# An encoder's FFN: the first two hidden units of each layer are computed like the others, their token differences are formed while the output projection ends, and the last rows' inputs are fetched earlier

## The chip, the cores and the metric

The kernel runs on 1 core of a Trainium2 chip. The time is that of the device in microseconds (us), from three runs; lower is better. The core's engines are TensorE (PE in the profile, with its weight loads as PEld), VectorE (DVE), ScalarE (ACT), GpSimd (POOL) and SyncE (SP). DMAs are issued from SP's, POOL's and, for a few, ACT's queue.

## What is computed

Two layers on 1024 tokens of width 1024, in float32. Each layer has a token mixer (layer 0: window attention; layer 1: a bidirectional gated linear recurrence; both with four cross-attention heads), an output projection, and an FFN, every part with a norm before and after it. The change lies in the FFN and in the end of the output projection.

```python
def conv_ffn(v, w_in, conv_w, conv_b, w_out):
    gate, up = jnp.split(v @ w_in, 2, axis=-1)
    hid = jax.nn.gelu(dwconv_centred(gate, conv_w, conv_b)) * up
    return hid @ w_out
```

w_in is 1024 x 5632 and w_out 2816 x 1024. The convolution runs over tokens, width 3.

## The kernel before

A float32 product is made of three matmuls: each operand is split in a high part (uh, wh; a cast on ACT) and a low part (ul, wl; a subtraction on DVE), and high x high, high x low and low x high are summed in PSUM.

**The FFN's first projection** runs over 22 units f of 128 hidden channels (gate and up together). For 20 of them (f from 2) a Strassen scheme cuts tokens, model width and gate/up in halves each: 7 products instead of 8, each 4 blocks of 128 x 3 matmuls of 128x512, into PSUM tiles X, Y and V (line 541, in mmk). The tokens' halves are i and j. The products' token operands are B[1], B[2], B[3] and B[5] to B[7] with B[4]: B1 to B3 are slices of uh and ul; B5 replaces the slice of the j half, lower four blocks, by a difference to the i half, and B4, B6 and B7 (u4, u6, u7, high and low each) are sums of the others, formed by operands() on DVE. The weights' operands are a raw slice (st), sx and sy (sums of slices, accumulated by DMAs on POOL's queue, lines 636 to 638, from loads on SP's queue, lines 633 and 634) and a second raw slice (a22). sx and sy have two buffers each, so units overlap in pairs.

Units 0 and 1 of each layer are computed by plain(): four PSUM tiles of 8 blocks x 3 matmuls. While PE works on them, operands() runs.

**In front of it** WOut.finish goes over eight row tiles of 128 tokens: the output projection into pb (lines 84 to 86), a norm, the residual (x, line 516), its store to h1d (line 517), and norm_T (line 115 makes nu, line 119 transposes it into pt; the split gives uh and ul). Small norm steps go over POOL (prs and nrs, line 96). PE works through its list in order; SP's, POOL's and ACT's DMAs are issued in the order of each queue, and an issue that waits holds up what is behind it.

**The FFN's second projection** runs seven products in the order 1, 6, 7, 4, 2, 5, 3 over 11 pairs of units, with loads st<-hid and st<-w2s on SP's queue. tail() ends a row tile: it reads the residual x back from h1d (line 800), norms, adds and stores; the first four row tiles during product 5, the last four behind product 3.

What stands in which order on each engine is decided by a scheduler that lists the instructions by their dependencies and priorities; its clock is a model.

Of the kernel before, what the change touches and what calls it, by code (L numbers as in the profile page):

```python
# [6 lines left out]
F32 = mybir.dt.float32  # L7
# [37 lines left out]
PLAIN = 2  # L45

# [3 lines left out]
def build(tc, A, out):  # L50
# [37 lines left out]
    def split(h, l, src):  # L88
        act.copy(h, src)  # L89
        dve.tensor_tensor(l, src, h.bitcast(F32), op=ALU.subtract)  # L90
# [19 lines left out]
    def norm_T(pl, pst, src, g, dh, dl, t, tag="n"):  # L110
        ss = pl.tile([P, 1], F32, tag=tag + "ss", name=tag + "ss")
        u = pl.tile([P, D], F32, tag=tag + "u", name=tag + "u")
        sumsq(pl, src, ss, u)
        rs = rstd_of(pl, ss, 1, D, tag)
        dve.scalar_tensor_tensor(u, src, rs[:, 0:1], g, op0=ALU.mult, op1=ALU.mult)
        for b in range(2):
            ps = pst.tile([P, 4, P], F32, tag="pt", name="pt")
            for k in range(4):
                pe.transpose(ps[:, k, :], u[:, (4 * b + k) * P:(4 * b + k + 1) * P], ident)
            split(dh[:, 4 * b:4 * b + 4, t * P:(t + 1) * P],  # L120
                  dl[:, 4 * b:4 * b + 4, t * P:(t + 1) * P], ps)
# [252 lines left out]
    class WOut:  # L374
# [96 lines left out]
        def finish(self):  # L471
            l = self.l
            self.wf = tc.alloc_tile_pool(name=f"wf{l}", bufs=1, side="right", reuse_waits="tile") if l == 0 else None
# [26 lines left out]
            self.first = wunit(A["ffw1"][l, 0, :, :1024], pl=self.wf) if l == 0 else None  # L500
            for t in self.order:
                pool.tensor_tensor(y0[:, t, :], y0[:, t, :], g1[:, :512], op=ALU.mult)
            for t in self.order:
# [8 lines left out]
                dve.tensor_tensor(y1, ps, g1[:, 512:], op=ALU.mult)  # L512
# [31 lines left out]
    def ffn(l, wo, dst, gnext, halves_, out_halves):  # L544
        u2p = tc.alloc_tile_pool(name=f"u2{l}", bufs=1, reuse_waits="tile")
# [6 lines left out]
        ncw = fp.tile([P, NF, 3], F32, name="ncw")  # L552
        dve.tensor_scalar_mul(ncw, cw, -1.0)
# [23 lines left out]
        def gtile():  # L577
            return fp.tile([P, T], F32, tag="g", bufs=1, name="g")

        def plain(f):  # L580

            wg = wo.first if f == 0 and wo.first else wunit(A["ffw1"][l, f, :, :1024])
            wu = wunit(A["ffw1"][l, f, :, 1024:])
            bank = lambda t: psx.tile([P, 512], F32, tag=t, name=t)
            gi, ui, gj, uj = bank("X"), bank("Y"), bank("V"), bank("Y")
            for (wh, wl), ps, m in ((wg, gi, ti), (wu, ui, ti), (wg, gj, tj), (wu, uj, tj)):
                mmk(ps, KT, lambda k: (wh[:, k * P:(k + 1) * P], wl[:, k * P:(k + 1) * P]),
                    lambda k: (uh[:, k, m], ul[:, k, m]), True)
            g = gtile()
            u = fp.tile([P, T], F32, tag="u", bufs=1, name="u")  # L590
            for gp, up_, m in ((gi, ui, ti), (gj, uj, tj)):
                act.activation(g[:, m], gp, AF.Copy, scale=-1.0)
                act.copy(u[:, m], up_)
            return conv(f, g, u)

        def operands():

            b12 = (uh[:, :4, tj], ul[:, :4, tj])
            late = []
            for kk in range(2):  # L600
                ks = slice(2 * kk, 2 * kk + 2)
                f32 = lambda x: x[:, ks].bitcast(F32)
                def tmp(t, b=1):
                    return fp.tile([P, 2, 512], F32, tag=t, bufs=b, name=t)
                def both(o, x, y, sub):
                    q = tmp("tt", 2)
                    dve.tensor_tensor(o, f32(x[0]), f32(y[0]), op=ALU.subtract)
                    dve.tensor_tensor(q, f32(x[1]), f32(y[1]), op=ALU.subtract)
                    dve.tensor_tensor(o, o, q, op=ALU.add)
                def more(o, a_, x, op):  # L610
                    dve.tensor_tensor(o, a_, f32(x[0]), op=op)
                    dve.tensor_tensor(o, o, f32(x[1]), op=op)
                x = tmp("c", 3)
                both(x, B[3], b12, True)
                split(B[7][0][:, ks], B[7][1][:, ks], x)
                more(x, x, B[1], ALU.add)
                nsplit(B[6][0][:, ks], B[6][1][:, ks], x)
                more(x, x, B[2], ALU.subtract)
                split(B[4][0][:, ks], B[4][1][:, ks], x)
                e1 = tmp("u") if kk else tmp("g")  # L620
                both(e1, B[1], b12, True)
                late.append((ks, e1))
            return late

        def load(f):

            w = A["ffw1"][l, f]
            a1 = stg.tile([P, 1024], F32, tag="st", name="st")
            a22 = stg.tile([P, 1024], F32, tag="st", name="st")[:, :512]
            sx, sy = [fp.tile([P, 1024], F32, tag=t, bufs=2, name=t) for t in ("sx", "sy")]  # L630
            nc.sync.dma_start(a1, w[:, 1024:])
            for c in range(2):
                nc.sync.dma_start(sx[:, c * 512:(c + 1) * 512], w[:, :512])
            nc.sync.dma_start(sy, w[:, 1024:])
            nc.sync.dma_start(a22, w[:, 512:1024])
            pool.dma_start(sx, w[:, 512:1536], accum_op=ALU.add, max_dma_last_dim=8192)
            pool.dma_start(sy[:, :512], sx[:, :512], accum_op=ALU.add, max_dma_last_dim=8192)
            pool.dma_start(sy[:, 512:], sy[:, :512], accum_op=ALU.add, max_dma_last_dim=8192)
            return a1, sx, sy, a22

        def weights(raw):

            for src in raw:
                n = src.shape[-1]
                h, l_ = [ring.tile([P, 1024], F32R, tag=t, name=t)[:, :n] for t in ("wh", "wl")]
                split(h, l_, src)
                yield h, l_
# [36 lines left out]
        def first_units():  # L684
            for f in range(PLAIN):
                c = plain(f)
                if f == 0:
                    late = operands()
                hidden(f, c)
                if f == PLAIN - 1:  # L690
                    for ks, e1 in late:
                        split(B[5][0][:, ks], B[5][1][:, ks], e1)
            raws = {f: load(f) for f in (PLAIN, PLAIN + 1)}
            gen = weights(raws.pop(PLAIN))
            ops = list(gen)
            X = [psx.tile([P, 512], F32, tag="X", name="X")]
            s = {}
# [7 lines left out]
            start(ops)  # L705
            yield
            for f in range(PLAIN, NF):
# [10 lines left out]
                v, y = (psx.tile([P, 512], F32, tag=t, name=t) for t in "VY")  # L718
                w = lambda k: operand(ops, k)
                prod(2, w(2), y, True)  # L720
# [17 lines left out]
                if f + 1 < NF:  # L738
                    X.append(psx.tile([P, 512], F32, tag="X", name="X"))
                    start(nxt)  # L740
# [5 lines left out]
                yield  # L746

# [27 lines left out]
        psx.release()  # L775
        fp.release()
        u2p.release()
        if wo.wf:
            wo.wf.release()
# [10 lines left out]
        y = {q: yp.tile([P, 4, 512], F32, name=q) for q in ("c11", "c21", "c12", "c22")}  # L790
# [37 lines left out]
        for k in SECOND:  # L828
# [4 lines left out]
            for p in range(NP2):  # L833
# [472 lines left out]
```

## Time and profile before

| | us |
|---|---|
| median of three runs | 2729.53 |
| lowest, highest | 2729.33, 2731.97 |
| profiled execution's span | 2732.3 |
| first projection's start, layer 0 | 593.4 to about 640 |
| first projection's start, layer 1 | about 2079 to 2125 |
| second projection's last product, layer 0 | from 1207.3 |
| second projection's last product, layer 1 | from 2690.9 to 2723.1 |

No time of the profiled execution apart from its span is given. Times in rows are microseconds from the start of the span, in groups the mean of one instruction is in ns. A row's bracket gives the idle time of its engine before it and what ended that. PE's records overlap, as matmuls are pipelined; the distance between starts is what one costs.

### The profile page before, as it was taken

How to read it: one execution, taken by the hardware profiler on the slowest of the kernel's cores; microseconds unless marked ns; L12 is line 12 of the kernel's file. 1: busy time of each engine (PE TensorE's matmuls, PEld its weight loads, DVE VectorE, ACT ScalarE, POOL GpSimd, SP SyncE). 2: the span in 40 equal slices, each digit the busy share in tenths (PEclk: the TensorE clock that was granted, in tenths of full speed). 3: DMA queues.
4: the chain of work that ended last, by engine and by line, in shares of the span. 5: the costliest groups of instructions: out<-in, count | busy, mean ns of one | idle time of the engine just before them, and what ended most of it. 6: DMA issues, size and time to landing. Idle time of an engine off the chain costs nothing.

```text
span 2732.3 us, 37483 instructions
## 1 busy us (share of the span) xinstructions
PE 2661.3 (97%) x13496; PEld 2231.1 (82%) x13496; DVE 1824.4 (67%) x3031; ACT 1391.2 (51%) x2550; POOL 468.6 (17%) x517
## 2 busy tenths in 40 slices
PE   8999999999999999999999999999899999999998
PEld 7888887788888888877888888888788788888886
DVE  6588777678556565488686767868566856556456
ACT  6367667544444445455444545545454544444453
POOL 1231120211111100032222231312121111110012
PEclk9999999999999999999999999999999999999999
DMA  8683213656777856673235531111466677775656
GB/s 282 207 186 75 66 49 97 204 183 154 199 205 187 206 155 232 204 249 124 86 124 127 117 78 55 55 47 34 133 219 170 165 202 204 197 206 159 222 192 219
DMA packets 213579, 428.45 MB, mean 157 GB/s; under 512 B 20368, under 2 KB 77072, under 8 KB 207760
## 3 DMA queue, kind: packets, MB, share of 16 engines
q1 hardware_dynamic: 187264, 333.50, 37.8%
q0 software_dynamic: 23680, 88.09, 15.6%
q10 hardware_dynamic: 2448, 4.46, 0.4%
q8 instruction: 106, 1.74, 0.3%
q14 instruction: 81, 0.66, 0.1%
HBM read 333.17 MB, written 117.96 MB: 165 GB/s over the span
## 4 chain that ended last, share of the span: by engine, by line
PE 84%; DVE 8%; DMA 3%; ACT 2%; issue 2%; POOL 1%; SPq 0%; DVEq 0%; POOLq 0%; ACTq 0%
PE X L541 25%; PE V L541 11%; PE pj L84 7%; PE pj L85 7%; PE pj L86 7%; PE Y L541 5%; PE pb L84 4%; PE pb L85 4%; PE pb L86 3%; PE po L1122 1%; PE pt L341 1%; PE pa L1074 1%; PE pa L1054 1%; DVE wl L80 1%; DVE wl L90 1%
## 5 line engine op out<-in xcount | busy, mean ns | idle before, releaser
L90 DVE TENSOR_TENSOR wl<-st,wh 128x1024 fp32r<-128x1024 f32 (+1 forms) x234 | 258.6, 1110 | 338.3 <-ACT wh L89 331.1
L89 ACT CAST wh<-st 128x1024 fp32r<-128x1024 f32 (+1 forms) x234 | 219.1, 938 | 291.4 <-PE X L541 180.4
L84 PE MATMUL pj<-uh,wh 128*128 128x512 f32 x512 | 206.6, 404 | 6.4 <-DVE xl L90 4.6
L541 PE MATMUL X<-wl,wh 128*128 128x512 f32 x528 | 205.6, 391 | 0.6 <-DVE wl L90 0.6
L541 PE MATMUL X<-wh,wl 128*128 128x512 f32 x528 | 205.7, 391 | 0.0
L541 PE MATMUL X<-wh 128*128 128x512 f32 x528 | 201.0, 391 | 4.0 <-DVE c L850 3.8
L86 PE MATMUL pj<-uh,wl 128*128 128x512 f32 x512 | 203.4, 398 | 0.0
L85 PE MATMUL pj<-ul,wh 128*128 128x512 f32 x512 | 202.7, 396 | 0.1
L84 PE MATMUL pj<-wh,uh 128*128 128x384 f32 (+1 forms) x512 | 190.2, 372 | 0.4 <-DVE v L283 0.4
L85 PE MATMUL pj<-wl,uh 128*128 128x384 f32 (+1 forms) x512 | 186.3, 364 | 0.0
L86 PE MATMUL pj<-wh,ul 128*128 128x384 f32 (+1 forms) x512 | 186.1, 364 | 0.0
L80 DVE TENSOR_TENSOR wl<-st,wh 128x1024 fp32r<-128x1024 f32 (+1 forms) x93 | 115.9, 1252 | 28.0 <-ACT wh L79 27.1
L541 PE MATMUL V<-uh,wh 128*128 128x512 f32 x344 | 133.9, 389 | 0.3 <-ACT uh L89 0.3
L541 PE MATMUL V<-ul,wh 128*128 128x512 f32 x344 | 134.0, 389 | 0.0
L541 PE MATMUL V<-uh,wl 128*128 128x512 f32 x344 | 133.9, 389 | 0.0
L79 ACT CAST wh<-st 128x1024 fp32r<-128x1024 f32 (+1 forms) x103 | 104.0, 1016 | 49.0 <-PE pj L85 27.2
L541 PEld LDWEIGHTS X<-wh 128*128 128x128 f32 x528 | 99.5, 189 | 25.9 <-issue 4.6
L84 PEld LDWEIGHTS pj<-uh,wh 128*128 128x128 f32 x512 | 97.3, 190 | 26.6 <-DVE xl L90 5.5
L1068 POOL TENSOR_TENSOR E<-EP,q 128x256 f32<-128x256 f32 x64 | 54.4, 851 | 372.0 <-DVE EP L1061 286.7
L541 PEld LDWEIGHTS X<-wl,wh 128*128 128x128 f32 x528 | 99.5, 189 | 21.9 <-DVE wl L90 1.0
L541 PEld LDWEIGHTS X<-wh,wl 128*128 128x128 f32 x528 | 99.4, 188 | 20.9
L86 PEld LDWEIGHTS pj<-uh,wl 128*128 128x128 f32 x512 | 97.0, 190 | 19.6
(337 smaller groups left out, 7328.7 us busy)
## 6 DMA issues: line engine op xcount, KB each, us to landing
st<-hid SPq DMA_DIRECT2D x154, 256.0 KB, 3.4
st<-in_ffw_dram SPq DMA_DIRECT2D x106, 256.0 KB, 3.5
w2s<-in_ffw_dram POOLq DMA_DIRECT2D x24, 1024.0 KB, 8.0
st<-in_ffw_dram SPq DMA_DIRECT2D x48, 512.0 KB, 3.7
hid<-tt SPq DMA_DIRECT2D x88, 256.0 KB, 4.6
st<-w2s SPq DMA_DIRECT2D x88, 256.0 KB, 3.2
sx<-in_ffw_dram SPq DMA_DIRECT2D x80, 256.0 KB, 4.0
sy<-in_ffw_dram SPq DMA_DIRECT2D x40, 512.0 KB, 5.8
```

The lines of the kernel that those rows point to most:

```text
L79: act.copy(h[:, :n], raw)
L80: (eng or dve).tensor_tensor(l[:, :n], raw, h[:, :n].bitcast(F32), op=ALU.subtract)
L84: pe.matmul(o, ah, bh, start=first, stop=False)
L85: pe.matmul(o, ah, bl, start=False, stop=False)
L86: pe.matmul(o, al, bh, start=False, stop=last)
L89: act.copy(h, src)
L90: dve.tensor_tensor(l, src, h.bitcast(F32), op=ALU.subtract)
L341: pe.transpose(tp[:, j, :], sm[:, j, c * P:(c + 1) * P], ident)
L541: pe.matmul(o, x, y, start=new, stop=e, skip_group_check=not first)
L1054: pe.matmul(pa[:, c, :], E2[:, cs], E1[:, cs], start=True, stop=True)
L1068: pool.tensor_tensor(gl, pl_, ql, op=ALU.mult)
L1074: pe.matmul(pa[eo:eo + n, c, lo:lo + n], G[:, c * P + eo:c * P + eo + n], G[:, c * P + lo:c * P + lo + n], start=True, stop=True, tile_pos ...
```

## The change

plain() is gone; all 22 units take 7 products. Units 0 and 1 run in step: products 1 and 2 of both, then (with products 1 and 2 of unit 2) product 5 of both, then 6, 3, 7 and 4. PSUM gets three X tiles, two Y and two V. WOut.finish forms the token differences in its last four row tiles: norm_T gets diff, adds high and low of the other half's tile on POOL (dw), subtracts the transposed tile from it on DVE, splits the difference in place (that is B5), and forms a second sum (xd) from which operands() makes u6, u7 and u4 with fewer steps. The raw loads of units 0 to 2 and the accumulating loads of 0 and 1 get a high priority; the last two stores to h1d are issued from ACT. In the second projection the x of the last four row tiles is fetched at the end of product 5 into y's buffers c11 and c21.

```diff
-    def norm_T(pl, pst, src, g, dh, dl, t, tag="n"):
+    def norm_T(pl, pst, src, g, dh, dl, t, tag="n", diff=None):
...
+        if diff:
+            x, oi = diff
+            w = pl.tile([P, 4, P], F32, tag="dw", bufs=2, name="dw")
+            pool.tensor_tensor(w, dh[:, :4, oi].bitcast(F32), dl[:, :4, oi].bitcast(F32), op=ALU.add)
...
+            if diff and b == 0:
+                dve.tensor_tensor(w, w, ps, op=ALU.subtract)
+                split(*d, w)
+            else:
+                split(*d, ps)
+            if diff and b == 1:
+                dve.tensor_tensor(x, ps, w, op=ALU.add)
...
-                nc.sync.dma_start(h1d[l][ts_, :], x)
-                norm_T(wp, psp, x, g2, uh, ul, t)
+                (act if n >= 6 else nc.sync).dma_start(h1d[l][ts_, :], x)
+                c = (n - 4) * P
+                self.mark = norm_T(wp, psp, x, g2, uh, ul, t,
+                       diff=(xd[:, :, c:c + P], slice(oi + c, oi + c + P)) if n >= 4 else None)
...
+            kk = [slice(0, 2), slice(2, 4)]
+            f32 = lambda k, c, ks: B[k][c][:, ks].bitcast(F32)
+            for ks in kk:
+                nsplit(B[6][0][:, ks], B[6][1][:, ks], wo.xd[:, ks])
+            yield
+            for k, o in ((1, 7), (2, 4)):
+                for ks in kk:
+                    x = fp.tile([P, 2, 512], F32, tag="tt", bufs=2, name="tt")
+                    dve.tensor_tensor(x, wo.xd[:, ks], f32(k, 0, ks), op=ALU.subtract)
+                    dve.tensor_tensor(x, x, f32(k, 1, ks), op=ALU.subtract)
+                    split(B[o][0][:, ks], B[o][1][:, ks], x)
...
-            for f in range(PLAIN):
-                c = plain(f)
...
+            with tc.high_priority(AHEAD):
+                a1 = [raw(A["ffw1"][l, f, :, 1024:]) for f in range(2)]
+                a22 = raw()
+                raws = {f: load(f, a1[f], a22[:, f * 512:(f + 1) * 512]) for f in range(2)}
+                a1.append(raw(A["ffw1"][l, 2, :, 1024:]))
...
+            for f in range(3):
+                with behind(wo.mark[:1] if f == 2 else []):
+                    prod(1, operand(us[f], 1), X[f], True)
+                    y = ys[f] if f < 2 else bank("Y")
+                    prod(2, operand(us[f], 2), y, True)
+                s1 = fp.tile([P, 512], F32, tag="s1", bufs=1, name="s1")
+                act.copy(s1, X[f])
+                if f < 2:
+                    dve.tensor_tensor(u[f][:, ti], y, s1, op=ALU.add)
...
+            for f in range(2):
+                prod(5, operand(us[f], 5), V[f], True)
+                act.copy(s5[f], V[f])
+            with behind(last_load):
+                raws[2] = load(2, a1[2])
+                raws[3] = load(3)
+            for f in range(2):
+                prod(6, operand(us[f], 6), X[f], False)
+                act.copy(u[f][:, tj], X[f])
...
-            x = np_.tile([P, D], F32, tag="x", bufs=2, name="x")
-            nc.sync.dma_start(x, h1d[l][ts_, :])
+            if b == ib:
+                x = xs[t // 2][:, t % 2, :]
+            else:
+                x = np_.tile([P, D], F32, tag="x", bufs=2, name="x")
+                nc.sync.dma_start(x, h1d[l][ts_, :])
...
+            if k == 5:
+                xs = [yp.tile([P, 2, D], F32, tag=q, name="x") for q in ("c11", "c21")]
+                for t in range(4):
+                    nc.sync.dma_start(xs[t // 2][:, t % 2, :], h1d[l][tok(ib, t), :])
```

PE at the start of layer 0's first projection, before; the rows shown are those at which the kind of product changes (pt is the transposed row tile, X, Y and V the PSUM tiles, uh the tokens' high part, xwh and wh weights' high parts):

```order
L119 MATMUL pt<-ident,nu 128x128 x8
L541 MATMUL X<-uh,xwh 128x512
...
L541 MATMUL Y<-uh,wh 128x512
...
L541 MATMUL X<-uh,wh 128x512
L119 MATMUL pt<-ident,nu 128x128 x8
L541 MATMUL X<-ul,wh 128x512
...
L541 MATMUL V<-uh,xwh 128x512
```

The same place in the changed kernel:

```order
L132 MATMUL pt<-ident,nu 128x128 x8
L564 MATMUL X<-uh,wh 128x512
...
L564 MATMUL Y<-uh,wh 128x512
...
L132 MATMUL pt<-ident,nu 128x128 x8
L564 MATMUL X<-uh,wh 128x512
...
L564 MATMUL V<-uh,wh 128x512
...
L564 MATMUL X<-u6h,wh 128x512
```

Between the last two row tiles' transposes stand 48 matmuls of units 0 and 1 where 49 of the plain unit 0 stood, and u6 is used 49 rows after the last transposes; before, u6 came first behind both plain units.

POOL's queue at the same place, before (nrs and prs are the small norm steps of the last row tiles, sx and sy the weight sums):

```order
L96 TENSOR_TENSOR prs<-pms,nhalf 128x1
L96 TENSOR_TENSOR nrs<-nms,nhalf 128x1
L636 DMA sx<-in_ffw_dram 128x1024 x2
L637 DMA sy<-sx 128x512 x2
L638 DMA sy<-sy 128x512 x2
L636 DMA sx<-in_ffw_dram 128x1024
```

And in the changed kernel:

```order
L128 TENSOR_TENSOR dw<-uh,ul 128x512
L102 TENSOR_TENSOR prs<-pms,nhalf 128x1
L102 TENSOR_TENSOR nrs<-nms,nhalf 128x1
L641 DMA sx<-in_ffw_dram 128x1024 x2
L642 DMA sy<-sx 128x512 x2
L643 DMA sy<-sy 128x512 x2
L641 DMA sx<-in_ffw_dram 128x1024 x2
```

The accumulating loads that follow the last row tile's nrs are now those of units 0 and 1, with those of units 2 and 3 behind them as a second pair; before, the first pair was that of units 2 and 3.

DVE at the end of the kernel, before (y is a row tile's evacuation from X and its scaling, x the last step of a row tile; numbers are buffers):

```order
L856 TENSOR_TENSOR y_24094<-X,c_22503 128x512
L858 TENSOR_TENSOR y_24094<-y_24094,g_22498 128x512
L802 TENSOR_TENSOR sq<-sb,q_22507 128x1
L94 TENSOR_SCALAR pms<-sq 128x1
L806 SCALAR_TENSOR_TENSOR x<-y_24094,prs,x 128x512
L806 SCALAR_TENSOR_TENSOR x<-c_22504,prs,x 128x512
L856 TENSOR_TENSOR y_24141<-X,c_22503 128x512
```

And in the changed kernel:

```order
L926 TENSOR_TENSOR y_24152<-X,c_22559 128x512
L928 TENSOR_TENSOR y_24152<-y_24152,g_22554 128x512
L868 TENSOR_TENSOR sq<-sb,q_22563 128x1
L926 TENSOR_TENSOR y_24197<-X,c_22559 128x512
L100 TENSOR_SCALAR pms<-sq 128x1
L872 SCALAR_TENSOR_TENSOR x<-y_24152,prs,x 128x512
L872 SCALAR_TENSOR_TENSOR x<-c_22560,prs,x 128x512
```

The last row tile's evacuation now stands ahead of the pms and x steps of the row tile before it.

More of the change, by code (lines that the diff above doesn't have):

```diff
@@ L1 @@
+from contextlib import ExitStack
 import numpy as np
@@ L43 @@
 HOLD = (4, 7)
-PLAIN = 2
 AHEAD = 2000
@@ L88, in split, with behind @@
     def split(h, l, src):
-        act.copy(h, src)
-        dve.tensor_tensor(l, src, h.bitcast(F32), op=ALU.subtract)
+        return act.copy(h, src), dve.tensor_tensor(l, src, h.bitcast(F32), op=ALU.subtract)
+    def behind(marks):
+        s = ExitStack()
+        for x in marks:
+            s.enter_context(tc.issue_after(x.ins))
+        return s
     def rstd_of(pl, ss, n, count, tag):
@@ L118, in norm_T @@
             for k in range(4):
-                pe.transpose(ps[:, k, :], u[:, (4 * b + k) * P:(4 * b + k + 1) * P], ident)
-            split(dh[:, 4 * b:4 * b + 4, t * P:(t + 1) * P],
-                  dl[:, 4 * b:4 * b + 4, t * P:(t + 1) * P], ps)
+                mark = pe.transpose(ps[:, k, :], u[:, (4 * b + k) * P:(4 * b + k + 1) * P], ident)
+            d = [x_[:, 4 * b:4 * b + 4, t * P:(t + 1) * P] for x_ in (dh, dl)]
+            if diff and b == 0:
[5 more added lines that the diff above has]
+                dve.tensor_tensor(x, ps, w, op=ALU.add)
+        return mark, made
     w2sum = [dram.tile([NP2, 4, P, 512], F32, name=f"w2s{l}") for l in range(2)]
@@ L499, in finish @@
             self.load(1)
-            self.first = wunit(A["ffw1"][l, 0, :, :1024], pl=self.wf) if l == 0 else None
             for t in self.order:
                 pool.tensor_tensor(y0[:, t, :], y0[:, t, :], g1[:, :512], op=ALU.mult)
-            for t in self.order:
+            for n, t in enumerate(self.order):
                 ts_ = slice(t * P, (t + 1) * P)
@@ L552, in ffn @@
         ncw = fp.tile([P, NF, 3], F32, name="ncw")
+        for t, n, b in (("g", T, 1), ("u", T, 1), ("c", T, 3), ("tt", T, 2), ("s1", 512, 1), ("sx", T, 2), ("sy", T, 2),
+                        ("s5", 512, 1), ("su", 512, 1)):
+            fp.tile([P, n], F32, tag=t, bufs=b, name=t)
+        u2p = tc.alloc_tile_pool(name=f"u2{l}", bufs=1, reuse_waits="tile")
         dve.tensor_scalar_mul(ncw, cw, -1.0)
@@ L578, in gtile @@
             return fp.tile([P, T], F32, tag="g", bufs=1, name="g")
[L580 to L594, printed above, removed]
@@ L596, in operands @@
-        def operands():
[L598 to L623, printed above, removed]
@@ L627, in load, with raw @@
+        def raw(src=None):
+            x = stg.tile([P, 1024], F32, tag="st", name="st")
+            if src is not None:
+                nc.sync.dma_start(x, src)
+            return x
+        last_load = [None]
+        def load(f, a1=None, a22=None):
             w = A["ffw1"][l, f]
-            a1 = stg.tile([P, 1024], F32, tag="st", name="st")
-            a22 = stg.tile([P, 1024], F32, tag="st", name="st")[:, :512]
+            if a1 is None:
+                a1 = raw(w[:, 1024:])
+            if a22 is None:
+                a22 = raw()[:, :512]
@@ L684, in first_units @@
         def first_units():
-            for f in range(PLAIN):
-                c = plain(f)
[L687 to L696, printed above, removed]
@@ L697, in first_units @@
-            s = {}
+            with tc.high_priority(AHEAD):
[3 more added lines that the diff above has]
+                a1.append(raw(A["ffw1"][l, 2, :, 1024:]))
+            gens = [weights(raws.pop(f)) for f in (0, 1)]
+            us = [[], []]
+            psv = [None]
+            bank = lambda t: (psv[0] if t == "V" else psx).tile([P, 512], F32, tag=t, bufs=3 if t == "X" else 2, name=t)
@@ new lines, in first_units, with nx @@
+            X, ys = [bank("X") for _ in range(3)], [bank("Y") for _ in range(2)]
+            u = [fp.tile([P, T], F32, tag=t, bufs=n, name="u") for t, n in (("u", 1), ("c", 3))]
+            s5 = [fp.tile([P, 512], F32, tag=t, bufs=1, name="s5") for t in ("s5", "su")]
+            def nx(f):
+                us[f].append(next(gens[f]))
+            nx(0)
+            nx(1)
+            with behind(wo.mark[1:]):
+                us.append(list(weights(a1[2:])))
+            for f in range(3):
[7 more added lines that the diff above has]
+                    dve.tensor_tensor(u[f][:, ti], y, s1, op=ALU.add)
@@ new lines, in first_units @@
+            nx(0)
+            nx(1)
+            make = operands()
+            with behind(last_split[0]):
+                next(make)
+            nx(0)
+            nx(1)
+            with behind(last_split[0]):
+                next(make)
+            psv[0] = tc.alloc_tile_pool(name=f"ffpv{l}", bufs=2, space=PSUM, reuse_waits="tile")
+            V = [bank("V") for _ in range(2)]
+            for f in range(2):
+                prod(5, operand(us[f], 5), V[f], True)
+                act.copy(s5[f], V[f])
@@ new lines, in first_units @@
+            with behind(last_load):
[4 more added lines that the diff above has]
+                act.copy(u[f][:, tj], X[f])
+            for f in range(2):
+                prod(3, operand(us[f], 3), V[f], False)
+                dve.tensor_tensor(u[f][:, tj], V[f], u[f][:, tj], op=ALU.add)
+            g = [gtile(), wo.xp.tile([P, T], F32, tag="xd", name="g")]
+            for f in range(2):
+                prod(7, operand(us[f], 7), X[f], False)
+                nx(f)
+                act.copy(g[f][:, tj], X[f])
+                dve.tensor_tensor(g[f][:, tj], g[f][:, tj], s5[f], op=ALU.add)
@@ L699, in start @@
+            gen = weights(raws.pop(2)[1:])
+            ops = us[2] + [next(gen)]
+            for f in range(2):
+                prod(4, operand(us[f], 4), X[f], False)
+                ops.append(next(gen))
+                act.copy(g[f][:, ti], X[f])
+            for f in range(2):
+                hidden(f, conv(f, g[f], u[f]))
+            X = X[2:]
+            s = {1: s1}
             def start(units):
@@ L703, in start @@
                 act.copy(s[1], X[-1])
-            start(ops)
             yield
-            for f in range(PLAIN, NF):
+            for f in range(2, NF):
                 if f + 2 < NF:
@@ L717, in first_units @@
                 x = X.pop()
-                v, y = (psx.tile([P, 512], F32, tag=t, name=t) for t in "VY")
+                v = bank("V")
                 w = lambda k: operand(ops, k)
-                prod(2, w(2), y, True)
+                if f > 2:
+                    y = bank("Y")
+                    prod(2, w(2), y, True)
                 u = fp.tile([P, T], F32, tag="u", bufs=1, name="u")
@@ L738, in first_units @@
                 if f + 1 < NF:
-                    X.append(psx.tile([P, 512], F32, tag="X", name="X"))
+                    X.append(bank("X"))
                     start(nxt)
@@ L789, in ffn @@
         dve.tensor_scalar_mul(g3[:, 512:], g3[:, 512:], -1.0)
-        y = {q: yp.tile([P, 4, 512], F32, name=q) for q in ("c11", "c21", "c12", "c22")}
+        y = {q: yp.tile([P, 4, 512], F32, tag=q, name=q) for q in ("c11", "c21", "c12", "c22")}
         ss = {q: yp.tile([P, 4], F32, name=q) for q in ("q11", "q21", "q22")}
```

21 lines of the change are left out of this document (11 added, 10 removed).

## The prediction

> **What bounds the kernel now.** I read the page first, then the chain of waits, then a table of stretches. The page's first row gives the busy time of each engine, the first row of its chain the share of each:
>
> ```profile
> PE 2661.3 (97%) x13496; PEld 2231.1 (82%) x13496; DVE 1824.4 (67%) x3031; ACT 1391.2 (51%) x2550; POOL 468.6 (17%) x517
> PE 84%; DVE 8%; DMA 3%; ACT 2%; issue 2%; POOL 1%; SPq 0%; DVEq 0%; POOLq 0%; ACTq 0%
> ```
>
> TensorE (PE) is busy for all but 71 of 2732.3 us, so time is won by taking matmuls away or by closing one of PE's few gaps, and lost by opening a gap. Two pieces of the chain between 680 and 712 us give the price of a matmul and the period of a unit; two stretches (length, then busy time of PE, weight load, DVE, ACT and POOL, clock, DMA share, GB/s) show where there are gaps:
>
> ```profile
> 692.50 5.44 PE X L541 x24
> ...
> 711.53 0.68 PE X L541 x3
> 594.00:692.50 98.50, 98.05 (x436) 80.31 (x435) 71.23 (x75) 43.02 (x56) 13.28 (x16) 1.00 0.65 163
> 711.53:1007.00 295.47, 295.47 (x1306) 244.64 (x1305) 174.85 (x189) 133.11 (x171) 37.22 (x43) 1.00 0.74 192
> ```
>
> 24 matmuls of 128x512 take 5.44 us, 0.2267 each. (The 391 ns "mean of one" in the groups is longer because matmuls overlap.) From 692.50 to 711.53 one whole unit passes, 19.03 us or 84 matmuls. The second stretch is the steady loop: no idle PE at all. The first is the start of the first layer's first projection, which the change rewrites in both layers. The gaps there and just ahead, by PE's waits from 2015 to 2180 us, the second layer's; from 480 to 700 us, in the first layer, the rows on nu and s read the same and the other two are not there (waiting and awaited line, total us, times, longest):
>
> ```profile
> PE X L541 <- DVE u6l L565: 0.9, 1, 0.9
> PE pt L119 <- DVE nu L115: 0.9, 1, 0.9
> PE X L541 <- ACT s L703: 0.4, 1, 0.4
> PE V L541 <- ACT uh L89: 0.3, 1, 0.3
> ```
>
> **Part 1: matmuls that go.** A plain unit has 4 banks x 8 blocks x 3 = 96 matmuls, a seven-product unit 7 x 4 x 3 = 84. Two units in each layer change: 24 matmuls a layer, 24 x 0.2267 = 5.44 us, **-10.9 us** in both. PE is the bound around them, so this comes through whole unless new gaps open.
>
> **Part 2: old gaps that go.** The two waits on s L703 (0.4 each), u6l and uh belong to the old entry into the unit loop, which no longer exists: -0.4 and -1.6. The wait on nu stands before the transposes of the last row tile but one and is closed in part only: DVE had a weight step of 1.22 us in front of nu, and now has xd, about 0.69 (the 128x512 row below). That is -0.5 a layer. Sum: **-0.9 and -2.1**.
>
> ```profile
> 590.86 1.22 DVE L80 TENSOR_TENSOR wl<-st,wh 128x1024 fp32r<-128x1024 f32 x1
> 593.42 1.06 PE L119 MATMUL pt<-ident,nu 128*128 128x128 f32 x8 [0.92 <-DVE nu L115]
> 594.24 0.48 PE L541 MATMUL X<-uh,xwh 128*128 128x512 f32 x1
> 594.32 0.69 DVE L512 TENSOR_TENSOR y<-pb,g 128x512 f32<-128x512 f32 x1
> 606.86 1.29 DVE L90 TENSOR_TENSOR ul<-pt,uh 128x512 fp32r<-128x512 f32 x2 [5.01 <-ACT uh L89]
> ```
>
> **Part 3: new gaps.** The plain units gave PE 43.5 us (192 matmuls) in which DVE formed the operand sums and GpSimd (POOL) summed weights by accumulating DMAs. That cover goes. I walk PE's new order with the old durations, in the first layer's times. First matmul 594.24 - 0.5 = 593.7; 48 matmuls (units 0 and 1, products 1 and 2) end at 604.6; eight transposes (594.24 - 593.42 = 0.8) at 605.4.
>
> (a) Unit 2's product 1 takes 2.7, to 608.1. Its Y needs a bank that DVE frees, behind five steps on the last row tile: the pair of ul that ended at 608.1 before becomes dw, ul, xd, ul, each 0.6 to 0.7, and one add. I put the add's end at 608.8: **0.7 late** (0 to 2). (b) Product 5 starts at 611.5. Its wl stands behind the third copy on ACT, a cast (1.05) and a step of 1.22 on DVE, done at 612.9, where PE wants wl two matmuls on, at 612.0: **0.9 late** (0 to 2). Its 24 matmuls end at 617.8.
>
> (c) Product 6 needs the weight tile sy, and sy is the end of a chain: load sx, accumulate sx on POOL's queue, sy from sx, sy from sy. The POOL timeline of before at the first such pair, then at a single unit in the steady loop, the median times from issue to landing (600 to 640 us, then 700 to 740), and the cast (mean of one in ns behind the busy time):
>
> ```profile
> 599.99 0.55 POOL L96 TENSOR_TENSOR nrs<-nms,nhalf 128x1 f32<-128x1 f32 x1 [2.97 <-DVE nms L94]
> 607.25 0.94 POOL L636 DMA_DIRECT2D sx<-in_ffw_dram  x1 [6.71 <-DMA sx<-in_ffw_dram]
> 615.37 0.86 POOL L637 DMA_DIRECT2D sy<-sx  x1 [2.86 <-DMA sx<-in_ffw_dram]
> 619.84 0.86 POOL L638 DMA_DIRECT2D sy<-sy  x1
> 622.61 0.86 POOL L638 DMA_DIRECT2D sy<-sy  x1 [1.91 <-DMA sy<-sx]
> sx<-in_ffw_dram POOLq DMA_DIRECT2D x3, 512.0 KB, 6.6
> sy<-sx POOLq DMA_DIRECT2D x2, 256.0 KB, 3.8
> sy<-sy POOLq DMA_DIRECT2D x2, 256.0 KB, 3.6
> sx<-in_ffw_dram SPq DMA_DIRECT2D x6, 256.0 KB, 3.9
> ...
> 700.12 0.87 POOL L636 DMA_DIRECT2D sx<-in_ffw_dram  x1 [5.47 <-DVE tt L680]
> 713.22 0.86 POOL L638 DMA_DIRECT2D sy<-sy  x1 [3.09 <-DMA sy<-sx]
> sy<-sy POOLq DMA_DIRECT2D x2, 256.0 KB, 5.7
> L89 ACT CAST wh<-sx 128x1024 fp32r<-128x1024 f32 x4 | 4.2, 1045 | 4.7 <-PE V L541 2.5 <-PE Y L541 2.2
> ```
>
> In the new order POOL has the last row tile's nrs in front of the first accumulate, so the chain cannot begin before 599.99 + 0.55 - 0.5 = 600.0, however early the loads on SP are. From the first issue to sy's landing it was 619.84 - 607.25 + 3.6 = 16.2 us for the first unit of the pair. So sy is there at 616.2, cast (1.05) at 617.3 and its wl (1.22) made at 618.5; PE wants the cast at 617.8 and wl four matmuls on, at 618.7: **just in time, 0**. For the second unit it is 622.61 - 607.25 + 3.6 = 19.0: sy at 619.0, wl at 621.3, and PE, 24 matmuls later, wants it at 624.1, with 2.8 to spare. (d) Unit 2 repeats this. Its sx takes over unit 0's buffer, free once wl is made (612.9); a load of 3.9 lets the chain start at about 617.5, sy is there at 633.7 and cast at 634.8. PE comes to it after 72 matmuls, at 617.8 + 16.3 = 634.1: **0.7 late**. (e) In the same place wl of sx stands behind seven DVE steps, most of which form u7 and u4; steps of 1.22 leave it **1.3 late** (0 to 3).
>
> New gaps: 0.7 + 0.9 + 0 + 0.7 + 1.3 = **+3.6 a layer**, taken the same in the second layer, whose order there is the same. The steps they come from are known, the lateness of each is a difference of two sums of 20 to 40 us, so I keep 0 and 7 as ends.
>
> [...]
>
> **Part 4: output projection.** Four row tiles a layer get one POOL add (dw) and two DVE steps of 0.69 beside the split. An add of that shape on POOL and what DVE did beside it:
>
> ```profile
> 1210.55 1.30 POOL L818 TENSOR_TENSOR c<-c,g 128x512 f32<-128x512 f32 x1 [1.07 <-ACT junk L103]
> 1211.23 6.17 DVE L90 TENSOR_TENSOR wl<-st,wh 128x1024 fp32r<-128x1024 f32 x3
> 560.00:594.00 34.00, 33.08 (x166) 27.54 (x165) 26.92 (x44) 19.45 (x36) 3.84 (x7) 1.00 0.49 167
> ```
>
> Three wl took 6.17 instead of 3 x 1.22 = 3.7, held up beside POOL. At worst a tile costs DVE 1.3 + 2 x 0.69 = 2.7 us. DVE has 7 idle us in these 34, over two to three tiles: 0, at most 2.7 once at the last tile before the matmuls (+2.7 a layer). I take 0, because one weight step leaves the same place. The later subtractions shrink from 28 steps of 128x1024 in a layer to 14; they lie behind PE, except for (e).
>
> **Part 5: early fetch of x.** The FFN's second stage ends with four row tiles that read x back from h1d. The four 512 KB fetches now leave together, at the end of product 5, in front of weights for the last product (3) on the same SP queue. PE's waits there and the end of the kernel:
>
> ```profile
> 1207.34 0.47 PE L541 MATMUL X<-wh 128*128 128x512 f32 x1 [1.78 <-DVE c L850]
> 1220.92 0.50 PE L541 MATMUL X<-wl,wh 128*128 128x512 f32 x1 [0.61 <-DVE wl L90]
> 1253.88 0.66 PE L119 MATMUL pt<-ident,nu 128*128 128x128 f32 x4 [1.55 <-DVE ul L90]
> 2660.00:2733.00 73.00, 61.01 (x260) 49.37 (x258) 46.78 (x63) 26.34 (x41) 20.85 (x15) 0.93 0.62 216
> 2722.67 0.40 PE L541 MATMUL X<-wh,wl 128*128 128x512 f32 x1
> 2722.95 0.75 DVE L806 SCALAR_TENSOR_TENSOR x<-y,prs,x 128x512 f32<-128x512 f32 x1 [2.61 <-DMA x<-h1d]
> 2724.28 0.68 DVE L856 TENSOR_TENSOR y<-X,c 128x512 f32<-128x512 f32 x1
> ```
>
> For: the 1.55 us at 1253.88 may go, where the norm's last steps waited for x, and at the end DVE's evacuation at 2724.28 could follow the last matmul (2722.67 + 0.40 = 2723.07) at once, -1.2. But DVE's new order puts the third tile's x steps behind that evacuation, so the last steps keep their place: 0 there. Against: 1 MB more in front of the weights, at 216 GB/s 4.9 us; the row at 1220.92 says that PE is already just in time there in the first layer. Ends: -2.8 and +4.9. I take 0, since the loads are waited for by 0.61 only and fetches that move are not added.
>
> **Sum** against the profiled 2732.3 us: -10.9 - 0.9 - 2.1 + 3.6 + 3.6 + 0 = **-6.7**. The profiled span lies 2.8 us, 0.1%, above the median of the three runs (2729.53); I carry the difference over to that median: **2722.8 us**.
>
> **Rivals.** *No new gaps.* The links and DVE keep up; the walk's 3.6 vanish: 2722.8 - 7.2 = 2715.6. For: (a), (b) and (d) are below 1 us each. Against: four of them on a path without slack. 0.13. *The accumulating chain runs at the steady loop's pace.* 713.22 - 700.12 + 5.7 = 18.8 instead of 16.2: in (c) wl is 2.4 late, in (d) the cast 1.1 instead of 0.7; +2.8 a layer, 2728.4. For: the start's DMAs are nearly as busy (share 0.65 against 0.74). Against: the pair in the old start took 16.2. 0.15. *The fetch of x holds up weights.* +4.9 once, the second layer's has its gap elsewhere: 2727.7. 0.08.
>
> *Slower: the two units' chains do not overlap.* Place: POOL's queue at each layer's start. If unit 1's accumulates come only after unit 0's, its sy lands at 600.0 + 2 x 16.2 = 632.4 and wl is made at 634.7, where PE wanted it at 624.1: +10.6 a layer, 0.7 less as (d) is covered then: 2722.8 + 19.8 = 2742.6. It is slower than before once unit 1's sy lands 2.8 + 3.4 = 6.2 us later than 619.0 in both layers, by 0.2% from 8.9. For: each issue waits for the one before to land, in queue order. Against: the old pair overlapped, 3 us apart. 0.10 with its milder forms. [...] *The change does nothing* (the scheduler fills PE as before): the new order has 48 matmuls fewer, so 0.02.
>
> **Chances.** The forecast has 0.52, by itself 2718 to 2728. A measurement of this kernel tells 0.2%, 5.5 us, from no change: faster means below 2724.1, slower above 2735.0. Of the forecast's 0.52 I give 0.40 to faster. The pace rival gives 0.02 of its 0.15 to faster. Faster 0.40 + 0.13 + 0.02 = 0.55; same 0.12 + 0.13 + 0.08 + 0.02 = 0.35; slower 0.10. The range goes from below the no-gaps rival to the slow pace of the chain: 2714 to 2732.
>
> **What would show it.** Right: 84-matmul units from the first on; PE's idle at each start some 3 to 4 us, on u (Y's bank), wl of sx, wl of sy. Wrong: idle PE at X<-u6h on sy with the first accumulate much after 600 or links over 6.6 us; PE waiting on wl in the second stage beside the x fetches; nu late in the projection's last rows with POOL's dw beside it.

## The result, and the profile after

The changed kernel took 2746.38 us (median of 5 runs, 2744.43 to 2747.96) against 2730.46 (2729.33 to 2733.77): a ratio of 1.0057, 95% interval 1.0046 to 1.0068. It is slower by 0.6%, 24 us above the forecast and above the range. No rival had the slower matmuls, and the one with a slow chain priced it too low.

The page's row of engines (busy us, share of the span, instructions) for the changed kernel:

```profile
PE 2665.1 (97%) x13448; PEld 2225.2 (81%) x13448; DVE 1818.9 (66%) x3039; ACT 1398.6 (51%) x2558; POOL 489.5 (18%) x537
```

What its PE waited for (us in total, times, longest), from 480 to 720 us, which holds layer 0's start, and below the second line of dots from 2015 to 2200 us, layer 1's:

```profile
PE X L564 <- ACT wh L89: 5.5, 2, 4.8
...
PE pt L132 <- DVE nu L124: 0.5, 1, 0.5
PE V L564 <- DVE wl L89: 0.5, 1, 0.5
PE Y L564 <- DVE u L720: 0.5, 1, 0.5
...
PE X L564 <- ACT wh L89: 3.8, 2, 3.1
PE pt L132 <- DVE nu L124: 3.1, 1, 3.1
PE V L564 <- DVE wl L89: 0.5, 1, 0.5
PE Y L564 <- DVE u L720: 0.4, 1, 0.4
```

The records of PE fell by 48, as the change says, and yet PE's busy time rose from 2661.3 to 2665.1 us. So matmuls became slower, which no table of waits shows. The chain of work that ended last shows it, at the same 24 matmuls of every unit in the steady loop; first and last of 18 such rows of the changed kernel:

```profile
689.22 5.62 PE X L564 x24
...
1017.77 5.62 PE X L564 x24
```

Before, the row at 692.50 had 5.44 us for 24 and the period was 19.03. Now 24 take 5.62, and the period is (1017.77 - 689.22) / 17 = 19.33 us for the same 84 matmuls, 0.30 more. Taken apart by the starts of the matmuls' records, those whose moving operand (the one that is streamed, here a token operand) is u4, u6 or u7, 36 of a unit's 84, start 233.9 ns apart on average; those on uh and ul stay near 227 to 228.

The other part of the loss is the wait for wh in both layers, at the first use of sy. POOL's timeline of the changed kernel there, in layer 0 (start, us, instruction, idle time ahead of it):

```profile
602.78 0.55 POOL L102 TENSOR_TENSOR nrs<-nms,nhalf 128x1 f32<-128x1 f32 x1 [4.31 <-DVE nms L100]
603.49 1.85 POOL L641 DMA_DIRECT2D sx<-in_ffw_dram  x2 [0.16 <-DMA h1d<-x]
611.81 0.86 POOL L642 DMA_DIRECT2D sy<-sx  x1 [6.47 <-DMA sx<-in_ffw_dram]
615.51 0.86 POOL L642 DMA_DIRECT2D sy<-sx  x1 [2.84 <-DMA sx<-in_ffw_dram]
618.17 0.86 POOL L643 DMA_DIRECT2D sy<-sy  x1 [1.80 <-DMA sy<-sx]
619.59 0.86 POOL L643 DMA_DIRECT2D sy<-sy  x1 [0.55 <-DMA sy<-sx]
```

And two rows of its chain from 600 to 640 us (start, us, what):

```profile
618.17 6.35 DMA sy<-sy
...
624.59 1.05 ACT wh L89
```

The last row tile's nrs runs at 602.78 (before: 599.99), the first accumulate is issued at 603.49, and sy is there at 618.17 + 6.35 = 624.5. From issue to landing that is 21.0 us, where the prediction had 16.2. The rows of stretches from the second link's issue to the last one's landing (length, engines' busy time, clock, DMA share, GB/s), changed kernel first, then before, show that the DMA engines were busier around it:

```profile
611.81:624.52 12.71, 8.52 (x36) 6.09 (x34) 5.51 (x6) 5.14 (x7) 4.04 (x5) 1.00 0.90 207
...
615.37:623.70 8.33, 8.33 (x39) 6.82 (x38) 4.26 (x4) 3.96 (x5) 3.44 (x4) 1.00 0.71 125
```

PE stands still for 4.83 us, by its timeline:

```profile
625.69 0.80 PE L564 MATMUL X<-u6h,wh 128*128 128x512 f32 x1 [4.83 <-ACT wh L89]
```

Then it gets only part of its clock. Busy time by stretches (engines, then the granted clock, third from the end, the DMA share and GB/s):

```profile
619.90:639.20 19.30, 14.47 (x58) 11.40 (x57) 12.29 (x13) 6.89 (x9) 4.84 (x6) 0.91 0.85 196
632.00:640.00 8.00, 8.00 (x36) 6.51 (x35) 7.92 (x9) 3.73 (x5) 2.62 (x3) 1.00 0.71 166
```

A mean of 0.91 over 19.3 us is 1.7 us of work lost; from 632 on the clock is whole again (1.00). In layer 1 the same happens behind a gap of 3.09 us:

```profile
2116.03 0.50 PE L564 MATMUL X<-u6h,wh 128*128 128x512 f32 x1 [3.09 <-ACT wh L89]
...
2116.80:2120.20 3.40, 3.40 (x9) 2.33 (x8) 2.00 (x3) 1.04 (x1) 0.87 (x1) 0.51 1.02 228
```

So the granted clock was about half (0.51) for 3.40 us here, behind a gap of 3.09. Shorter gaps were followed by the same: in the profile of before the 2.06 us ahead of 2690.88 (0.50 from 2692.1 to 2695.5), in the changed kernel's the 2.09 us on nu ahead of 1265.46 (0.50 from 1266.9 to 1270.3). It wasn't each time: behind the 3.15 us on nu in layer 1, which end at 2087.36, the changed kernel's clock was 1.00 up to 2104. What decides it isn't shown.

The account against the profiled execution of before, by the rows of both (us): matmuls -10.9; slower streaming of 1584 matmuls x (233.9 - 226.8) ns = +11.2; waits at the starts, layer 0 7.0 for 1.3 = +5.7, layer 1 7.8 for 2.5 = +5.3; half clock behind both waits, 2 x 1.7 = +3.4; and at the last product of layer 1 a wait of 2.1 with a half-clock stretch (1.6) that the profile of before has and this one has not, -3.7. Sum +11.0; the spans differ by 2743.3 - 2732.3 = 11.0.

That they meet to a tenth is luck. From the first matmul of each stage to that of the next, the first projection took 8.7 us more in layer 0 and 6.1 in layer 1, where the items that lie in it give 8.0 and 5.0; ahead of, between and behind the two the differences are +1.9, -1.9 and -3.8, where the items give -0.4, +2.2 and -3.7. The +1.9 has nothing to do with the change: the execution was 2.1 us later already at about 117 us. Nor is the wait of 2.1 that went away at the end a gain of the change, as far as e2 and e8 (below) show, whose kernels are the one before but for some bytes: their profiles have none of it and 0.6 us.

The runs differ by 15.9, as the profiled execution of before was a late one: with the 1.75 us by which the changed kernel's profiled run (2745.05) is longer than its span, it stands at 2734.0, 3.6 above its median, and the changed kernel's is 1.3 below.

### The profile page after: what moved, and what is told of

Same layout as the page of the kernel before. It is cut to its first block, busy times and chain, and to the rows that moved or that the text cites. A ratio compares the mean times of both kernels' runs of the same rounds, so it can differ in the third digit from the quotient of the medians.

```text
span 2743.3 us, 37508 instructions
## 1 busy us (share of the span) xinstructions
PE 2665.1 (97%) x13448; PEld 2225.2 (81%) x13448; DVE 1818.9 (66%) x3039; ACT 1398.6 (51%) x2558; POOL 489.5 (18%) x537
## 4 chain that ended last, share of the span: by engine, by line
PE 87%; DVE 6%; DMA 3%; ACT 2%; issue 2%; POOL 1%; SPq 0%; DVEq 0%; POOLq 0%; ACTq 0%
PE X L564 29%; PE V L564 10%; PE pj L84 8%; PE pj L85 7%; PE pj L86 7%; PE Y L564 4%; PE pb L84 3%; PE pb L85 3%; PE pb L86 3%; PE po L1192 1%; PE pa L1144 1%; PE pt L361 1%; PE pa L1124 1%; PE pu L1168 1%; DMA sx<-in_ffw_dram 1%
```

## Experiments

Ratios are to the kernel before in runs on the same chip. Labels name what was edited.

### Is it where u4, u6 and u7 begin?

In the new order of the pools these tiles begin at byte 171328 of a partition instead of 119456. Theory A: a start of the moving operand on a multiple of 64 is slow (they began 32 beyond one before). Rival: the high addresses.

```diff
                         ("s5", 512, 1), ("su", 512, 1)):
             fp.tile([P, n], F32, tag=t, bufs=b, name=t)
+        fp.tile([P, 8], F32, name="pad")
         u2p = tc.alloc_tile_pool(name=f"u2{l}", bufs=1, reuse_waits="tile")
```

> The changed kernel with 32 unused bytes in front of the tiles u4, u6 and u7, so that they begin 32 bytes past a multiple of 64 (as before the change) and not on one; nothing else in the first projection's order moves. Theory A (a moving operand on a multiple of 64 bytes is streamed slower): products with u4, u6, u7 go from 233.9 to 226.8 ns a matmul, 1584 x 7.1 ns = 11.2 us less, about 2735 us. Rival B (the high addresses of these tiles, above 171328, or the traffic there are slow): they stay at 233.9 and the time at 2746.

Measured: 2746.86 us, ratio 1.0066 (1.0051 to 1.0081): no gain; 24 matmuls on u took 5.60 us.

The counterpart moves the same tiles by 32 bytes in the kernel before, at their old, low place:

```diff
+        u2p.tile([P, 8], F32, name="pad")
         for k in (4, 6, 7):
             B[k] = tuple(u2p.tile([P, 4, 512], F32R, name=f"u{k}{c}") for c in "hl")
+        u2p.tile([P, 8], F32, name="pad2")
```

> The kernel before with 32 unused bytes in front of u4, u6 and u7 (and 32 behind them), so that they begin on a multiple of 64 at the same low addresses. Theory A: 1440 matmuls at 234 instead of 226.8 ns, 10.3 us more, about 2741 us. Rival B: no change, 2730.

Measured: 2743.69 us, ratio 1.0049 (1.0033 to 1.0065); one of its five executions took 12908.5 us and isn't in the ratio. Two rows of its chain in the steady loop, both of 24 matmuls on u:

```profile
706.17 5.60 PE X L541 x24
...
725.53 5.60 PE X L541 x24
```

32 bytes alone make the kernel before slower by 0.5%, with no matmul added: the period is 725.53 - 706.17 = 19.36 us. So high addresses are not needed, the rival falls for this kernel; but by e1 the start modulo 64 isn't the rule either.

### The rule, by matmuls alone

> Only groups of 96 matmuls of 128x512 on float32r, one group for each start of the moving operand (l: low addresses, h: high ones, m: bytes past a multiple of 64) and of the stationary one (s); no other engine works beside them but for evacuations. The encoder is left out. Theory A: m32 at 226.7 ns, m0 at about 234, in l and h alike, m16 and m48 unknown. Rival B: l all at 226.7, h slower. Rival C (it is a collision with other engines' accesses and not the start alone): all groups at 226.7.

The chain of waits gives each group's time (one start of the moving operand and one of the stationary, that is the weights that are loaded; l and h the place, m the start, s isn't printed: the first four of l have s 32, the next four s 0; of h the first two rows shown have s 32, the last has s 0):

```profile
54.39 21.53 PE lm32s L43 x95
75.93 21.93 PE lm0s L43 x94
97.86 22.40 PE lm16s L43 x96
...
142.50 22.39 PE lm32s L43 x96
164.89 21.79 PE lm0s L43 x96
...
276.10 22.30 PE hm32s L43 x96
298.40 22.41 PE hm0s L43 x96
...
365.38 22.49 PE hm32s L43 x96
```

32 with 32 (21.53 / 95 = 226.6 ns) and 0 with 0 (227.0) are fast, 32 with 0 and 0 with 32 slow (233.2, 233.3). It isn't the one start but the two together, and with nothing else running, so no collision with other engines. The high tile was slow throughout, but it lay 128 bytes beyond a multiple of 512 from the weights. (Its last row shown is at 128 + 32 = 160 bytes, as u4 to u7 are in the changed kernel: 22.49 / 96 = 234.3 ns.) Hence theory C: the distance between the two operands counts.

> Only matmul groups of 96, as in e3, the encoder is left out; now the stationary start is fixed and m is the distance of the moving start to it beyond a multiple of 512 (low: 0 to 2048; high: 0, 128, 512, with the high tile itself a multiple of 512 away). Theory C (after e3, where 32/32 and 0/0 were fast and 32/0, 0/32 slow in the low tile and all were slow in the high tile, which lies 170624 bytes = 128 beyond a multiple of 512 away): what counts is the distance between the two operands modulo 512; m 0, 512, 1024, 2048 at 226.7 ns, all others at about 233, and h as l. Rival B: h slow whatever m is. Rival D (modulus 4096): 512, 1024 and 2048 slow too.

```profile
53.75 21.33 PE lm0s L43 x94
75.08 22.17 PE lm32s L43 x95
97.25 21.97 PE lm64s L43 x96
...
164.04 22.39 PE lm192s L43 x96
186.43 21.78 PE lm256s L43 x96
208.21 21.99 PE lm320s L43 x96
...
340.21 21.76 PE hm0s L43 x96
361.97 22.39 PE hm128s L43 x96
384.36 21.79 PE hm512s L43 x96
```

Distances of 0, 256 and 512 (and 1024, 2048) take 226.7 to 227.0 ns a matmul, low or high; 64 and 320 take 229, the others 232 to 233. So theory C holds with a smaller modulus: 256, not 512. In the kernel before all of uh, ul, the weights' tiles and u4 to u7 lay multiples of 512 apart, but for two weights' tiles of layer 0's first plain unit (xwh and xwl, 192 beyond, 48 matmuls). The change put u4 to u7 160 beyond one, e1 192. So the profile of before had the slow pace too, at the place from which the prediction took its first matmul, PE's timeline there:

```profile
594.55 0.40 PE L541 MATMUL X<-ul,xwh 128*128 128x512 f32 x1
...
599.69 0.40 PE L541 MATMUL X<-uh,xwl 128*128 128x512 f32 x1
```

These are 22 matmuls from start to start, 5.14 / 22 = 233.6 ns each, where the steady loop had 226.7.

### The rule in the kernels

e6 is e1 with `[P, 88]` for `[P, 8]`, 352 bytes; e8 is e2 with `[P, 128]` in front and nothing behind.

> The changed kernel with 352 unused bytes in front of u4, u6 and u7, which puts them a multiple of 512 from the weights' tiles. Theory C: their products at 226.8 ns, 1584 x 7.1 ns = 11.2 us less than the changed kernel, about 2735. Rival B (high addresses): no change, 2746.

> The kernel before with 512 unused bytes in front of u4, u6 and u7, a control for e2: shifted further, but by a multiple of 512. Theory C: no change, 2728 to 2731. Rival (any shift of these pools costs, by other orders or waits): 2735 or more.

Measured: e6 2738.05 us, ratio 1.0022 (1.0013 to 1.0031); e8 2729.82, ratio 0.9996 (0.9987 to 1.0005). First and last of 18 rows in e6's steady loop:

```profile
688.75 5.44 PE X L564 x24
...
1012.43 5.44 PE X L564 x24
```

5.44 us for 24 is back, the period is (1012.43 - 688.75) / 17 = 19.04 us. By the ratios e6 wins back 0.35% of the changed kernel's time, 9.6 us of the 11.2 expected. e8 shows that a shift as such costs nothing.

### The wait for sy

```diff
+            if f < 2:
+                pool.tensor_tensor(sy[:, :512], sy[:, :512], sx[:, :512], op=ALU.add)
+                pool.tensor_tensor(sy[:, 512:], sy[:, 512:], sy[:, :512], op=ALU.add)
+            else:
...
```

> As e1_shift32, and for units 0 and 1 of each layer sy is summed by two adds of 128x512 on POOL (1.3 us each) in place of two accumulating DMAs (6.4 and about 4 us). Theory (the accumulating chain is what PE waits for at product 6): the waits on the cast of sy (5.5 and 3.8 us) fall below 1 us each, and the two half-clock stretches behind them (1.7 us each) go: 11 to 12 us less than e1, about 2723. Rival (u6's low part on DVE or the casts on ACT are as late): 0 to 4 us less than e1.

Measured: 2737.37 us, ratio 1.0039 (1.0026 to 1.0052), 9.5 us less than e1 by the medians and 0.27%, 7.4 us, by the ratios, against 11 to 12 expected. The waits on wh were 5.0 and 1.9 us in e1's profile, less than the 5.5 and 3.8 that the expectation took; in e4's there is none in layer 0 and 0.8 in layer 1. What PE waits for in layer 0 now, beside 1.3 us on nu:

```profile
PE X L564 <- ACT u4h L89: 0.7, 1, 0.7
PE V L564 <- DVE wl L89: 0.5, 1, 0.5
PE Y L564 <- DVE u L725: 0.5, 1, 0.5
```

So in layer 0 the chain of accumulating DMAs was what PE waited for, and the next step behind it costs less than 1 us. In layer 1 another stood close behind: there PE's waits on wl rose from 0.5 us in e1 to 1.7 in e4.

> e6 with e4's adds on POOL in place of the accumulating DMAs to sy of units 0 and 1. The two causes add: 2737.4 (e4) less 11.2 us, about 2726, faster than before by 0.1 to 0.2%. Rival (without the slow streaming PE only waits the more at the starts): 2730 or more.

Measured: 2728.97 us (11 runs), ratio 0.9987 (0.9978 to 0.9995): with both causes out, the changed kernel is faster than before by 0.13%, 3.6 of the 6.7 us that were forecast. Within the intervals the two add: without the slow streaming the chain costs 0.35% (e6 less e7), with it 0.27% (e1 less e4); the streaming costs 0.35% with the chain (the changed kernel less e6) and 0.52% without (e4 less e7).

### POOL's dw and the wait for nu

The wait on nu in layer 1 (3.1 us) is left in e7. The changed kernel's timeline there, POOL's row of dw and DVE's of that nu:

```profile
2084.87 1.26 POOL L128 TENSOR_TENSOR dw<-uh,ul 128x512 f32<-128x512 f32 x1
2084.93 2.28 DVE L124 SCALAR_TENSOR_TENSOR nu<-x,nrs,g 128x1024 f32<-128x1024 f32 x1 [0.44 <-POOL nrs L102]
```

nu took 2.28 us (2.27 in e7), where it took 1.27 to 1.29 elsewhere. dw begins 0.06 us ahead of nu and ends at 2086.13, 1.20 into it; nu is 1.0 longer, about the time that the two run side by side. e9 and e10 take dw away from there: e9 is e7 with `bufs=3` for dw, e10 is e7 with the add on `dve`.

> e7 with three buffers for dw instead of two, so that POOL's add for the last row tile no longer waits for the split of the row tile two before and stands earlier in POOL's queue. Theory (in layer 1 PE waits 3.1 us on nu because POOL's dw runs beside nu, which took 2.28 instead of 1.27 us, and because the tile's nrs comes late): that wait falls by 1 to 2 us, about 2727. Rival (the steps dw, ul and xd on DVE ahead of nms are what delays it): 3 us as before, 2729.

> e7 with the add dw on DVE (0.68 us, four a layer) instead of POOL. Theory of e9: nu back at 1.27 us, layer 1's wait on nu down by about 1 us, layer 0's unchanged at 0.5; 2728. Rival: the four adds on DVE, in order with the norm's steps, cost as much: 2729 to 2731.

Measured: e9 2726.04 us, ratio 0.9981 (0.9972 to 0.9990); e10 2726.76, ratio 0.9981 (0.9972 to 0.9990). In e9's trace, DVE's timeline:

```profile
2072.49 1.28 DVE L124 SCALAR_TENSOR_TENSOR nu<-x,nrs,g 128x1024 f32<-128x1024 f32 x1 [0.44 <-POOL nrs L102]
```

And PE's waits from 2015 to 2200 us:

```profile
PE pt L132 <- DVE nu L124: 2.2, 1, 2.2
```

With dw out of its way nu is back at 1.28 and the wait falls from 3.1 to 2.2 us, about as much as nu became shorter. Where the rest comes from isn't shown: the steps dw, ul and xd ahead of nms on DVE were the rival, but in e10, with dw's add on DVE as well, the wait in layer 1 is shorter still, 1.4. In layer 0 e10 has 1.4 for 0.5; e4, with its adds on POOL, had 1.3 there, so that need not be DVE's adds either. Against e7 neither gain is clear of the intervals; against before both kernels are faster by 0.19%.

### The early fetch of x

```diff
-            if b == ib:
-                x = xs[t // 2][:, t % 2, :]
-            else:
-                x = np_.tile([P, D], F32, tag="x", bufs=2, name="x")
-                nc.sync.dma_start(x, h1d[l][ts_, :])
+            x = np_.tile([P, D], F32, tag="x", bufs=2, name="x")
+            nc.sync.dma_start(x, h1d[l][ts_, :])
...
```

> e7 without the early fetch of x: the last four row tiles of the second projection read it one by one, as before. Prediction's value for that part was 0 (ends -2.8 and +4.9): 2728 to 2730, the second projection's 217.2 and 209.6 us of e7 within 1 us and the tail behind the last matmul at 9.8. If the fetch helps, the tail or the entry into the next layer gets longer by 1.2 to 2.8 us; if it holds up weights, the second projection gets shorter.

Measured: 2727.84 us, ratio 0.9987 (0.9978 to 0.9996), the same as e7. The wait at the entry into layer 1's mixer, by PE's waits from 1000 to 1270 us, is 1.2 us on ul for e7's 2.1 on nu and 0.5 on ul. The fetch neither helped nor hurt by an amount that the runs can tell. Its profile isn't a clean pair for e7's: the scheduler's order at layer 1's start differs too, and there PE waits 4.3 us on wh. From its first matmul to its last the second projection took 217.2 and 209.6 us in e7, 215.5 and 210.1 in e11, and the tail behind it 9.7 and 9.6. Over all profiles of kernels with the fetch the two layers took 215.4 to 217.2 and 209.6 to 210.6, over those without it 215.5 to 216.8 and 209.9 to 210.6 (213.5 in the one of before, with the wait named above), so no part of it shows an effect either.

## Why the prediction was wrong

**Part 1, the matmuls that go: the count right, the price of those that stay wrong.** 48 fewer are there. "PE is the bound around them, so this comes through whole unless new gaps open" left out that a matmul can change its price without a gap: the change moved u4, u6 and u7 in memory, and 1584 matmuls took 7.1 ns more each, +11.2 us, which is the whole gain. e2, e5, e6 and e8 show it. It was hard to see: the diff shows that the pool moved, and the profile of before had 48 matmuls at that pace, but nothing there tied the pace to the distance.

**Part 2, old gaps.** The four old waits went as said. The wait on nu came out at 0.5 in layer 0, close to the 0.4 that was left to it, and at 3.1 in layer 1 instead of 0.4: mis-sized by 2.7 us, of which 0.9 are the dw beside it (e9); the rest stays open.

**Part 3, new gaps.** (a) 0.5 and 0.4 for 0.7, (b) 0.5 for 0.9, (e) 0 for 1.3: near or too dear. (d) came out at 0.7 in both layers as forecast, but by luck: in layer 0 the chain of waits runs there not over the DMA but over ACT, whose cast of sx (642.64) and a copy (643.60) stand ahead of the cast of sy (644.07).

(c) is the step that failed: "just in time, 0" was 4.8 us in layer 0 and 3.1 in layer 1. The term that was mis-sized is the chain, 21.0 us for 16.2. Its first link took 8.3 us to the next one's issue, as in the rows that gave the 16.2 (8.1); the second and third took 6.4 each, for 4.5 and 3.6. The chain also began 3.5 us later than reckoned (603.5 for 600.0), but PE came 3.1 later too (620.9 for 617.8). Together 4.8 + 3.5 - 3.1, less the slack of 0.5, is 4.7; measured 4.83. That the links were slower because of the transfers beside them (DMA share 0.90 for 0.71) is a reading of the rows, not tested; that PE waited for these links is shown by e4 and e7, in layer 0 above all. The prediction's own sign of being wrong, idle PE at X<-u6h on sy with the first accumulate much after 600 or links over 6.6 us, is what came. The rival of the slow chain had the mechanism; its 18.8 us were still too few, and it had no half clock behind the wait.

**Part 4, output projection.** The value 0 was near. The last row tile's nrs ran 2.8 us later than before, but PE's first matmul of the first projection was 1.85 later itself (596.09 for 594.24), as the whole execution was; against PE it is 0.9, inside the bound of +2.7. It costs through (c), not at the place looked at.

**Part 5, the fetch of x: 0, right**, by e11 as far as the runs can tell.

**The slow clock behind a gap** was not priced: 1.7 us after each of the two long waits on wh, so the wait of 4.8 us cost 6.5.

The rival that ended slower, chains that do not overlap, did not happen: by POOL's rows above the second unit's links were issued 3.7 and 1.4 us behind the first's. Nor did GpSimd stand at an issue: the links to sy took 0.86 us to issue, as before.

## What to carry to other kernels

When a change touches the order or the size of pools, compare the addresses of what TensorE streams with those of the weights that it loads, and look at the starts of matmuls, not at their busy time: a loop with no idle time can still have become 1.6% slower. A pad that brings the two a multiple of 256 bytes apart settles it in one run, as e6 did (5.44 us for 24 matmuls, 5.62 without the pad); a pad that doesn't, as in e1 (5.60), leaves it open. A chain of DMAs that becomes the first thing a stage waits for is to be timed with the load that it will have there, from the last instruction ahead of it in its queue.

## What the runs showed of the hardware

A float32r matmul of 128x512 took 226.6 to 227.0 ns where the moving operand's start lay a multiple of 256 bytes from the stationary one's, 229 at 64 beyond (and 320), and 231 to 234.3 at the other distances tried (32, 96, 128, 160, 192, 384 and 448 among them), at low and high addresses. In these groups each matmul had its own weight load and the stationary slices were 512 bytes apart; other shapes and types weren't tried, and why the distance counts stays open. In the changed kernel's steady loop it was worth 7.1 ns a matmul (233.9 for 226.8).
